# Gated recurrence of eight heads: output kept channel by token, its norm's sums made by products with ones, and a new table of deadline shifts

## The chip, the cores and the metric

The kernel runs on one core of one Trainium2 chip. The metric is the device time of one execution in microseconds, as the median of several runs. The kernel before took 1561.24 us (three runs, 1560.71 to 1561.47).

## The reference

One layer of a hybrid decoder on 1024 tokens of width 2048. `x` is normalised and multiplied with a combined weight `w_in`; its columns go to three groups: spatial gating in chunks of 128 tokens (gMLP), a gated delta rule with 8 heads of 128 channels, and attention into 256 memory tokens with 4 heads. Each group's output is multiplied with SiLU of its own gate columns, the three are joined, multiplied with `w_out`, added to `x`, and normalised again. The part that the change touches is the delta rule:

```python
q = l2norm(to_heads(q)) * DN_HEAD_DIM ** -0.5
k = l2norm(to_heads(k))
...
q_g = q * jnp.exp(g_cum)[..., None]
...
def step(state, inp):
    qg_c, kcd_c, val_c, ai_c, kd_c, gl_c = inp
    v_new = val_c - jnp.einsum('bhid,bhde->bhie', kcd_c, state)
    o_c = jnp.einsum('bhid,bhde->bhie', qg_c, state) + jnp.einsum('bhij,bhje->bhie', ai_c, v_new)
    state = state * jnp.exp(gl_c)[..., None, None] + jnp.einsum('bhid,bhie->bhde', kd_c, v_new)
    return state, o_c
...
o = rmsnorm(o, dn_norm_g[l]) * jax.nn.silu(d_z.reshape(B, S, DN_HEADS, DN_HEAD_DIM))
```

So each head's output `o` is normalised over its 128 channels, token by token, and each query is normalised to length one before it is used. The kernel runs the recurrence in chunks of 128 tokens.

## The kernel before

All tiles have 128 partitions. The 1024 tokens are worked on in two halves `hf` of 512 (`HT`), each of four chunks `tt` of 128.

**The big products.** The input projection, the memory's keys and values and the output projection are products of 128x128 by 128x512. Each factor is split into a high part (a cast to fp32r, on ScalarE, `S`) and a low part (a subtraction on VectorE, `V`), and three products stand for one (`triple`). `seven` arranges the blocks so that seven block products do the work of eight, which costs additions and subtractions of blocks on VectorE. Weights come in chunks into `raw`, and their parts stand in `rhi` and `rlo`, two of each; the left factors in `lh`, `ll`, `lm`.

**The order of work** is neither the order of the code nor found at run time. `Plan` records every operation with a cost that `price` gives it by engine and shape, builds the dependences from the tiles that are read and written, computes a due time for each operation from the end backwards (`late`), and lays the operations out in a simulated run (`lay`), each engine taking the ready operation with the earliest due time. `SHIFT` is a table by hand: it adds so many nanoseconds to the due times of single operations, which it names by their number. The result is a fixed sequence for each engine; at run time an engine only waits for semaphores. SyncE (`Q`, in the profile SP) issues nearly all DMAs, in its own fixed order. For ScalarE the plan knows that Exp, Silu and Gelu each need their own table (`FITS`), and books a load of it.

**The recurrence** is done in two parts for each pair of heads `p` and half `hf`, and both are worked in between the big products.

- `front` (line 1230): `conv` makes keys and queries, channel by token (128 channels on the partitions, 512 tokens). `qk` (line 1000) turns the keys to token by channel in PSUM (`to_tokens`: four TensorE transposes of 128x128) and sums their squares (`sumsq`: four ScalarE instructions that each square 128 columns and write the sum of a row). It then turns the queries in the same way for the sums of their squares, `hs[:, 0]`. It forms the products of keys with keys and queries with keys, and at last multiplies the queries by the row of decays that a DMA has put into a tile `vs` from `ring["tn"]`. Queries, keys, `kd` and `ai` go to HBM (`late_d`), the two norms that are still needed go to `late_hs`.
- `inverse` and `levels` invert the triangular matrices of four pairs at a time.
- `front_late` (line 1247) loads the tiles again, `values` makes the values, `back` runs four times `scan_step` (line 1170) and then `heads_out` (line 1211). `back_of` (line 1647) calls them. Pairs 0 and 1 (heads 0 to 3) are worked during the second projection stage, pairs 2 and 3 during the third.

In `scan_step` the output of a chunk is made token by channel, with the queries and then `ai` as the stationary operand:

```python
PE.matmul(d0, q, s, start=True, stop=False)
PE.matmul(d0, ai, w, start=first, stop=True)
```

and copied into `vs`. In `heads_out` the squares of a token stand in one row, so `sumsq` sums them in four instructions; one small VectorE operation adds the queries' term, `rsqrt_to` takes the power -1/2 on GpSimd, `by_token` scales the four chunks by it on ScalarE. Four transposes then turn the output to channel by token, in the bank that the scan used, and it is read from PSUM, multiplied by `dn_norm_g` and, for heads 4 to 7, by their gate (`g_d`), or stored to `o_d` until the gate of heads 0 to 3 is there.

Of the kernel before, what the change touches and what calls it, by code (L numbers as in the profile page):

```python
# [11 lines left out]
F32R = mybir.dt.float32r  # L12
AF = mybir.ActivationFunctionType
ALU = mybir.AluOpType
# [4 lines left out]
P = 128  # L19
# [18 lines left out]
KP = 4  # L38
ON_ACT = (3,)
NEG = -1.0e30  # L40
FITS = {AF.Exp: 1, AF.Silu: 2, AF.Gelu_apprx_tanh: 3}

# [21 lines left out]
class Plan:  # L64
# [8 lines left out]
    FETCH = 3500.0  # L73
    TABLE, HOLD = 1300.0, 6000.0
    SHIFT = {
# [5 lines left out]
    }  # L81

    def __init__(self, nc):
# [340 lines left out]
def kernel(  # L424
# [101 lines left out]
    ring["E"] = Ring("E", 2, [P, HT])  # L526
    ring["tn"] = Ring("tn", 4, [P, HT])
    ring["xr"] = Ring("xr", 3, [P, HT + 3])
    ring["hs"] = Ring("hs", 4, [P, 10, NT])
    jk = C([P, HT], "jk", mybir.dt.bfloat16)  # L530
    gr = C([NT * NH, P], "gr")
    small = Ring("small", 8, [P, 8])
# [8 lines left out]
    def tpb():  # L541
# [9 lines left out]
    G.affine_select(out=ident, in_=ident, compare_op=ALU.not_equal, fill=1.0, base=0,  # L551
                    pattern=[[-1, P]], channel_multiplier=1)
    G.memset(ones, 1.0)
    mhalf = C([P, 8], "mhalf")
    G.memset(mhalf, -0.5)
    with rank(0):
# [443 lines left out]
    def qk(h, hf, tiles, hs, gt, bank):  # L1000

        q, k = tiles[:2]
        kd, ai, vs = map(tok, (*tiles[2:4], ring["tn"]()))
        beta, edk = (scs[hf][:, i] for i in (0, 4))
        (kt,) = to_tokens((k, bank))
        sumsq(hs[:, 1], kt)
        V.tensor_scalar(hs[:, 1], hs[:, 1], EPS, None, op0=ALU.add)
        V.reciprocal(hs[:, 3], hs[:, 1])
        V.scalar_tensor_tensor(hs[:, 2], hs[:, 3], -1.0, beta[:, :, h], op0=ALU.mult, op1=ALU.mult)
        V.tensor_tensor(out=hs[:, 3], in0=hs[:, 2], in1=edk[:, :, h], op=ALU.mult)  # L1010
        by_token(kd, kt, hs[:, 3])
        e = tok(ring["E"]())
        Q.dma_start(e.rearrange("p t c -> p (t c)"), e_d[hf][h])
        Q.dma_start(vs.rearrange("p t c -> p (t c)"), row_of(ecs[hf], h))
        by_token(e, e, hs[:, 2])
        (qt,) = to_tokens((q, bank))
        sumsq(hs[:, 0], qt)
        V.tensor_scalar(hs[:, 0], hs[:, 0], P * EPS, P * EPS * EPS, op0=ALU.mult, op1=ALU.add)
        rsqrt_to(hs[:, 4], hs[:, 1])
        V.tensor_tensor(out=hs[:, 4], in0=hs[:, 4], in1=hs[:, 1], op=ALU.mult)  # L1020

        ch, cl = (ring["inv"](F32R).rearrange("p (t s c) -> p t s c", s=2, c=P) for _ in range(2))
        for i, src in enumerate((k, q)):
            split_to(ch[:, :, i], cl[:, :, i], tok(src), V)
        for t2 in range(NT // 2):
            d = bank
            for j in range(2):
                tt = 2 * t2 + j
                triple(d[:, j * 2 * P : (j + 1) * 2 * P], (ch[:, tt, 0], cl[:, tt, 0]), (ch[:, tt], cl[:, tt]),
                       True, True, R.cls)  # L1030
            dv = d.rearrange("p (t s c) -> p t s c", s=2, c=P)
            ts = slice(2 * t2, 2 * t2 + 2)
            V.tensor_tensor(out=gt[:, ts], in0=dv[:, :, 0], in1=e[:, ts], op=ALU.mult)
            V.tensor_tensor(out=ai[:, ts], in0=dv[:, :, 1], in1=e[:, ts], op=ALU.mult)
        V.tensor_tensor(out=q, in0=q, in1=vs.rearrange("p t c -> p (t c)"), op=ALU.mult)

    def blocks_out(gt, n):

# [131 lines left out]
    def scan_step(hf, hp, tt, qs, ks, rest, ut):  # L1170
# [12 lines left out]
        with rank(1):  # L1183
# [11 lines left out]
            with R.together():  # L1195
                if not last:
                    for s, q, k, kd, ai, vs, u, d0, d1, r, w, e, n in heads:
                        PE.matmul(d1, kd, w, start=True, stop=True)
                for s, q, k, kd, ai, vs, u, d0, d1, r, w, e, n in heads:
                    if not first:  # L1200
                        PE.matmul(d0, q, s, start=True, stop=False)
                    PE.matmul(d0, ai, w, start=first, stop=True)
            for s, q, k, kd, ai, vs, u, d0, d1, r, w, e, n in heads:
                if first:
                    V.tensor_copy(s, d1)
# [2 lines left out]
            for s, q, k, kd, ai, vs, u, d0, d1, r, w, e, n in heads:  # L1208
                S.copy(vs, d0)

    def heads_out(hf, hp, hss, rest):
        obs = [vs for kd, ai, vs in rest]

        for hs, ob in zip(hss, obs):
            sumsq(hs[:, 5], ob)
            V.scalar_tensor_tensor(hs[:, 6], hs[:, 5], 1.0 / P, hs[:, 0], op0=ALU.mult, op1=ALU.add)
            rsqrt_to(hs[:, 7], hs[:, 6])
            by_token(ob, ob, hs[:, 7])
        for h, ob, bank in zip(hp, obs, scan_banks):
            (tp,) = to_tokens((ob.rearrange("p t c -> p (t c)"), bank))  # L1220
            if h < NJ:
                S.activation(ob, tp, AF.Copy, scale=col2[:, 8:9])
                Q.dma_start(tok(o_d[hf][h]), ob)
            else:
                e, y = ring["E"](), ob.rearrange("p t c -> p (t c)")
                Q.dma_start(e, g_d[hf][h - NJ])
                V.scalar_tensor_tensor(ob, tp, col2[:, 8:9], tok(e), op0=ALU.mult, op1=ALU.mult)
                head_done(h, hf, y)

    def front(p, hf, banks):  # L1230

# [2 lines left out]
        for i, h in enumerate(hp):  # L1234
# [1 line left out]
            conv(1, h, hf, tiles[1])  # L1236
            conv(0, h, hf, tiles[0])
            qk(h, hf, tiles, hs, gt[:, i], banks[i])
            V.tensor_copy(late_hs[:, hf, h], hs[:, 0:5:4])
            for d, t in zip(late_d[hf][h], tiles[:4]):  # L1240
                Q.dma_start(d, t)
        gdr = blocks_out(gt, f"{hf}{p}")
# [4 lines left out]
    def front_late(p, hf):  # L1247

        hp = (2 * p, 2 * p + 1)
        qs, ks, hss, rest = [], [], [], []  # L1250
        for h, tiles in zip(hp, back_sets):
            hss.append(ring["hs"]())
            V.tensor_copy(hss[-1][:, 0:5:4], late_hs[:, hf, h])
            for d, t in zip(late_d[hf][h], tiles):
                Q.dma_start(t, d)
            qs.append(tiles[0])
            ks.append(tiles[1])
            rest.append([tok(t) for t in tiles[2:]])
        return hf, hp, qs, ks, hss, rest

    def values(hf, hp, qs, ks, hss, rest):
        for i, h in enumerate(hp):
            v = ring["tn"]()
            conv(2, h, hf, v)
            bank = scan_banks[i]
            by_token(rest[i][2], to_tokens((v, bank))[0], hss[i][:, 4])

    def back(hf, hp, qs, ks, hss, rest, ut):
        for tt in range(NT):
            scan_step(hf, hp, tt, qs, ks, rest, ut)  # L1270
        heads_out(hf, hp, hss, rest)


    late_hs = C([P, 2, NH, 2, NT], "lhs")

    def halves(t):
        n = t.shape[1] // 2
# [363 lines left out]
    project_stage(heads_of(NJ), to_heads(NJ), made=yu_d[0] if NA > 0 else None)  # L1641
    inv = inverse(gdrs, gg_d[0], "a", 1.9)
    front_sets = over([own_set])
    scan_banks = [dnr.bufs[0]] * 2
    gdrs = []

# [107 lines left out]
    scan_banks = dnr.bufs[0:2]  # L1754
    hand = dnr.bufs[3]
    wide = acc
    el = over([abh[:, 0:HT], ring["tn"].bufs.pop()])
    for hf in range(2):
        spatial(hf)
# [331 lines left out]
```

## Time and profile before

| what | value |
|---|---|
| runs | 1561.24 us median, 1560.71 to 1561.47 |
| profiled execution | 1558.44 us, its span 1556.70 us |
| granted TensorE clock | 0.998 |
| instructions | 25174 |
| HBM | 336.58 MB read, 100.40 MB written |

The span reaches from the first to the last instruction of the profiled execution; the execution's time has what lies around it as well. Nearly all instructions are recorded on line 420, the place where the plan issues them, so groups of instructions are told apart by their tiles: `dn<-ident,vs` is an operation that reads `ident` and `vs` and writes a PSUM bank `dn`; the names on the right are sorted by the alphabet and don't tell which operand is stationary. `acc` and `dn` are the two sets of four PSUM banks. A row of groups has count, busy time, mean length in ns, and the idle time of the engine ahead of it with what ended it. An fp32 product of 128x128 has two records, a transpose one. Lengths of TensorE instructions overlap; what one costs is read from the distance of starts.

### The profile page before, as it was taken

How to read it: one execution, taken by the hardware profiler on the slowest of the kernel's cores; microseconds unless marked ns; L12 is line 12 of the kernel's file. 1: busy time of each engine (PE TensorE's matmuls, PEld its weight loads, DVE VectorE, ACT ScalarE, POOL GpSimd, SP SyncE). 2: the span in 40 equal slices, each digit the busy share in tenths (PEclk: the TensorE clock that was granted, in tenths of full speed). 3: DMA queues.
4: the chain of work that ended last, by engine and by line, in shares of the span. 5: the costliest groups of instructions: out<-in, count | busy, mean ns of one | idle time of the engine just before them, and what ended most of it. 6: DMA issues, size and time to landing. Idle time of an engine off the chain costs nothing.

```text
span 1556.7 us, 25174 instructions
## 1 busy us (share of the span) xinstructions
PE 1546.4 (99%) x8725; PEld 1299.2 (83%) x8725; DVE 1250.4 (80%) x1843; ACT 947.8 (61%) x1942; POOL 102.0 (7%) x125
## 2 busy tenths in 40 slices
PE   9999999999999999999999999999999999999997
PEld 8988888888888888888888888888888888888886
DVE  6966974777898946788789975878758999998996
ACT  7833385565874335698885454776557874464554
POOL 0100000100021000010111010010000000000000
PEclk9999999999999999999999999999999999999999
DMA  9999976999879797786797987999958999775984
GB/s 326 308 303 332 310 258 220 308 329 311 297 248 296 239 276 223 265 281 198 260 327 270 326 242 230 310 328 333 346 208 271 314 333 328 268 254 198 342 276 174
DMA packets 348642, 438.68 MB, mean 282 GB/s; under 512 B 78553, under 2 KB 183394, under 8 KB 348514
## 3 DMA queue, kind: packets, MB, share of 16 engines
q1 hardware_dynamic: 346930, 434.37, 85.4%
q0 software_dynamic: 1088, 2.10, 0.5%
q8 instruction: 69, 1.13, 0.3%
q10 hardware_dynamic: 496, 0.61, 0.1%
q14 instruction: 59, 0.48, 0.1%
HBM read 336.58 MB, written 100.40 MB: 281 GB/s over the span
## 4 chain that ended last, share of the span: by engine, by line
PE 95%; DVE 3%; issue 1%; ACT 1%; DMA 0%; POOL 0%; POOLq 0%; SPq 0%; DVEq 0%; ACTq 0%
PE acc L420 60%; PE dn L420 35%; DVE rlo L420 1%; DVE ll L420 0%; DVE tn L420 0%; DVE obs L420 0%; DVE raw L420 0%; DVE inv L420 0%; DMA raw<-in_w_mem_kv_dram 0%; ACT E L420 0%; DVE rs L420 0%; DVE kept L420 0%; DVE xa L420 0%; ACT lh L420 0%; DVE small L420 0%
## 5 line engine op out<-in xcount | busy, mean ns | idle before, releaser
L420 PE MATMUL acc<-lh,rhi 128*128 128x512 f32 x1024 | 395.4, 395 | 0.0
L420 PE MATMUL acc<-lh,rlo 128*128 128x512 f32 x1024 | 384.8, 396 | 0.0
L420 ACT CAST rhi<-raw 128x1024 fp32r<-128x1024 f32 (+1 forms) x145 | 183.3, 1265 | 210.1 <-PE dn L420 106.6
L420 DVE TENSOR_TENSOR rlo<-raw,rhi 128x1024 fp32r<-128x1024 f32 (+1 forms) x145 | 215.5, 1486 | 95.8 <-ACT rhi L420 83.7
L420 PE MATMUL acc<-ll,rhi 128*128 128x512 f32 x688 | 267.1, 395 | 0.1
L420 PEld LDWEIGHTS acc<-lh,rhi 128*128 128x128 f32 x1024 | 192.3, 188 | 37.0 <-ACT qT L420 0.2
L420 PEld LDWEIGHTS acc<-lh,rlo 128*128 128x128 f32 x1024 | 191.6, 188 | 37.0
L420 PEld LDWEIGHTS acc<-ll,rhi 128*128 128x128 f32 x688 | 129.2, 188 | 25.1 <-DVE ll L420 0.6
L420 DVE TENSOR_TENSOR ll<-ll,lh 128x1024 fp32r<-128x1024 f32 x105 | 128.3, 1222 | 11.0 <-ACT lh L420 10.3
L420 PE MATMUL acc<-lm,rhi 128*128 128x512 f32 x336 | 131.6, 394 | 0.0
L420 ACT CAST lh<-ll 128x1024 fp32r<-128x1024 f32 (+1 forms) x107 | 111.5, 1043 | 23.8 <-PE dn L420 9.7
L420 PE MATMUL dn<-lh,rhi 128*128 128x512 f32 x288 | 112.6, 393 | 0.0
L420 PE MATMUL dn<-lh,rlo 128*128 128x512 f32 x288 | 110.8, 394 | 0.0
L420 PE MATMUL dn<-ll,rhi 128*128 128x512 f32 x192 | 75.1, 392 | 0.0
L420 DVE TENSOR_TENSOR rlo<-kept,rhi 128x1024 fp32r<-128x1024 f32 (+1 forms) x38 | 52.7, 1389 | 25.6 <-ACT rhi L420 25.5
L420 PEld LDWEIGHTS acc<-lm,rhi 128*128 128x128 f32 x336 | 63.2, 188 | 12.0
L420 ACT CAST rhi<-kept 128x1024 fp32r<-128x1024 f32 (+1 forms) x38 | 45.3, 1192 | 42.7 <-PE acc L420 25.4
L420 DVE TENSOR_TENSOR raw<-raw,kept 128x1536 f32<-128x1536 f32 (+1 forms) x42 | 64.3, 1532 | 3.2 <-DMA raw<-in_w_in_dram 2.3
L420 POOL TENSOR_TENSOR hs<-hs,mhalf 128x4 f32<-128x4 f32 x32 | 45.8, 1433 | 298.1 <-DVE hs L420 298.1
L420 PEld LDWEIGHTS dn<-lh,rhi 128*128 128x128 f32 x288 | 54.2, 188 | 10.2
L420 PEld LDWEIGHTS dn<-lh,rlo 128*128 128x128 f32 x288 | 54.1, 188 | 10.4
L420 POOL TENSOR_TENSOR small<-small,mhalf 128x1 f32<-128x1 f32 x26 | 19.7, 758 | 634.4 <-DVE small L420 634.4
(500 smaller groups left out, 3460.1 us busy)
## 6 DMA issues: line engine op xcount, KB each, us to landing
raw<-in_w_in_dram SPq DMA_DIRECT2D x168, 256.0 KB
raw<-in_w_in_dram SPq DMA_DIRECT2D x72, 512.0 KB
raw<-in_w_out_dram SPq DMA_DIRECT2D x64, 512.0 KB
ll<-hsd SPq DMA_DIRECT2D x54, 512.0 KB
lm<-hsd SPq DMA_DIRECT2D x26, 512.0 KB
pd<-obs SPq DMA_DIRECT2D x48, 256.0 KB
late<-os SPq DMA_DIRECT2D x44, 256.0 KB
ll<-h0d SPq DMA_DIRECT2D x18, 512.0 KB
```

Of the source, the lines that this page charges most:

```text
L420: o.fn(*o.args, **o.kw)
```

## The change

- `scan_step`: the operands of the two products for the output change places, so that it comes out channel by token.
- `heads_out`: the squares of queries and output (each with its scale, as 512 columns) are added on VectorE, split into a high and a low part, and summed over the channels by two TensorE products with a 128x128 tile of ones, `ones_r`, so that each of the 128 partitions holds the sum. A VectorE reciprocal of 128x512 out of PSUM and a ScalarE square root follow, and one VectorE product. There are no turns of the output and no GpSimd power. The tiles of queries, keys, `kd` and `ai` are used as working space.
- `qk`: the queries aren't turned, their squares not summed, and their product with the decay row is left out; `front_late` makes it, with the row loaded into a tile `faded` of its own, since `heads_out` needs the queries without decay.
- `front_late` takes its tiles from the rings anew each time, instead of from two fixed sets.
- `hs` and `late_hs` are half as large, `ones_r` is new, and `FITS` has the square root as a fourth table.
- `SHIFT` has 60 entries in place of 32, nearly all of them others.

```diff
--- before.py
+++ after.py
@@ -38,7 +38,7 @@
 KP = 4
 ON_ACT = (3,)
 NEG = -1.0e30
-FITS = {AF.Exp: 1, AF.Silu: 2, AF.Gelu_apprx_tanh: 3}
+FITS = {AF.Exp: 1, AF.Silu: 2, AF.Gelu_apprx_tanh: 3, AF.Sqrt: 4}

@@ -73,11 +73,14 @@
     FETCH = 3500.0
     TABLE, HOLD = 1300.0, 6000.0
     SHIFT = {
...
     }

     def __init__(self, nc):
@@ -526,7 +529,7 @@
     ring["E"] = Ring("E", 2, [P, HT])
     ring["tn"] = Ring("tn", 4, [P, HT])
     ring["xr"] = Ring("xr", 3, [P, HT + 3])
-    ring["hs"] = Ring("hs", 4, [P, 10, NT])
+    ring["hs"] = Ring("hs", 4, [P, 5, NT])
     jk = C([P, HT], "jk", mybir.dt.bfloat16)
     gr = C([NT * NH, P], "gr")
     small = Ring("small", 8, [P, 8])
@@ -551,6 +554,9 @@
     G.affine_select(out=ident, in_=ident, compare_op=ALU.not_equal, fill=1.0, base=0,
                     pattern=[[-1, P]], channel_multiplier=1)
     G.memset(ones, 1.0)
+    ones_r = C([P, P], "onesr", F32R)
+    with rank(0):
+        S.copy(ones_r, ones)
     mhalf = C([P, 8], "mhalf")
     G.memset(mhalf, -0.5)
     with rank(0):
@@ -1000,7 +1006,7 @@
     def qk(h, hf, tiles, hs, gt, bank):

         q, k = tiles[:2]
-        kd, ai, vs = map(tok, (*tiles[2:4], ring["tn"]()))
+        kd, ai = map(tok, tiles[2:4])
         beta, edk = (scs[hf][:, i] for i in (0, 4))
         (kt,) = to_tokens((k, bank))
         sumsq(hs[:, 1], kt)
@@ -1011,11 +1017,7 @@
         by_token(kd, kt, hs[:, 3])
         e = tok(ring["E"]())
         Q.dma_start(e.rearrange("p t c -> p (t c)"), e_d[hf][h])
-        Q.dma_start(vs.rearrange("p t c -> p (t c)"), row_of(ecs[hf], h))
         by_token(e, e, hs[:, 2])
-        (qt,) = to_tokens((q, bank))
-        sumsq(hs[:, 0], qt)
-        V.tensor_scalar(hs[:, 0], hs[:, 0], P * EPS, P * EPS * EPS, op0=ALU.mult, op1=ALU.add)
         rsqrt_to(hs[:, 4], hs[:, 1])
         V.tensor_tensor(out=hs[:, 4], in0=hs[:, 4], in1=hs[:, 1], op=ALU.mult)

@@ -1032,7 +1034,6 @@
             ts = slice(2 * t2, 2 * t2 + 2)
             V.tensor_tensor(out=gt[:, ts], in0=dv[:, :, 0], in1=e[:, ts], op=ALU.mult)
             V.tensor_tensor(out=ai[:, ts], in0=dv[:, :, 1], in1=e[:, ts], op=ALU.mult)
-        V.tensor_tensor(out=q, in0=q, in1=vs.rearrange("p t c -> p (t c)"), op=ALU.mult)

     def blocks_out(gt, n):

@@ -1198,8 +1199,8 @@
                         PE.matmul(d1, kd, w, start=True, stop=True)
                 for s, q, k, kd, ai, vs, u, d0, d1, r, w, e, n in heads:
                     if not first:
-                        PE.matmul(d0, q, s, start=True, stop=False)
-                    PE.matmul(d0, ai, w, start=first, stop=True)
+                        PE.matmul(d0, s, q, start=True, stop=False)
+                    PE.matmul(d0, w, ai, start=first, stop=True)
             for s, q, k, kd, ai, vs, u, d0, d1, r, w, e, n in heads:
                 if first:
                     V.tensor_copy(s, d1)
@@ -1208,24 +1209,29 @@
             for s, q, k, kd, ai, vs, u, d0, d1, r, w, e, n in heads:
                 S.copy(vs, d0)

-    def heads_out(hf, hp, hss, rest):
-        obs = [vs for kd, ai, vs in rest]
-
-        for hs, ob in zip(hss, obs):
-            sumsq(hs[:, 5], ob)
-            V.scalar_tensor_tensor(hs[:, 6], hs[:, 5], 1.0 / P, hs[:, 0], op0=ALU.mult, op1=ALU.add)
-            rsqrt_to(hs[:, 7], hs[:, 6])
-            by_token(ob, ob, hs[:, 7])
-        for h, ob, bank in zip(hp, obs, scan_banks):
-            (tp,) = to_tokens((ob.rearrange("p t c -> p (t c)"), bank))
+    def heads_out(hf, hp, raw_q, ks, rest):
+
+        for h, q, k, (kd, ai, vs), bank in zip(hp, raw_q, ks, rest, scan_banks):
+            o = vs.rearrange("p t c -> p (t c)")
+            S.activation(q, q, AF.Square, scale=math.sqrt(P * EPS))
+            S.activation(k, o, AF.Square, scale=1.0 / math.sqrt(P))
+            V.scalar_tensor_tensor(q, k, EPS * EPS, q, op0=ALU.add, op1=ALU.add)
+            hi, lo = ring["kd"](F32R), ring["ai"](F32R)
+            split_to(hi, lo, q, V)
+            with R.together():
+                PE.matmul(bank, ones_r, hi, start=True, stop=False)
+                PE.matmul(bank, ones_r, lo, start=False, stop=True)
+            V.reciprocal(k, bank)
+            S.activation(k, k, AF.Sqrt)
+            V.tensor_tensor(out=o, in0=o, in1=k, op=ALU.mult)
             if h < NJ:
-                S.activation(ob, tp, AF.Copy, scale=col2[:, 8:9])
-                Q.dma_start(tok(o_d[hf][h]), ob)
+                S.activation(o, o, AF.Copy, scale=col2[:, 8:9])
+                Q.dma_start(o_d[hf][h], o)
             else:
-                e, y = ring["E"](), ob.rearrange("p t c -> p (t c)")
+                e = ring["E"]()
                 Q.dma_start(e, g_d[hf][h - NJ])
-                V.scalar_tensor_tensor(ob, tp, col2[:, 8:9], tok(e), op0=ALU.mult, op1=ALU.mult)
-                head_done(h, hf, y)
+                V.scalar_tensor_tensor(o, o, col2[:, 8:9], e, op0=ALU.mult, op1=ALU.mult)
+                head_done(h, hf, o)

     def front(p, hf, banks):

@@ -1236,7 +1242,7 @@
             conv(1, h, hf, tiles[1])
             conv(0, h, hf, tiles[0])
             qk(h, hf, tiles, hs, gt[:, i], banks[i])
-            V.tensor_copy(late_hs[:, hf, h], hs[:, 0:5:4])
+            V.tensor_copy(late_hs[:, hf, h], hs[:, 4])
             for d, t in zip(late_d[hf][h], tiles[:4]):
                 Q.dma_start(d, t)
         gdr = blocks_out(gt, f"{hf}{p}")
@@ -1247,31 +1253,34 @@
     def front_late(p, hf):

         hp = (2 * p, 2 * p + 1)
-        qs, ks, hss, rest = [], [], [], []
-        for h, tiles in zip(hp, back_sets):
-            hss.append(ring["hs"]())
-            V.tensor_copy(hss[-1][:, 0:5:4], late_hs[:, hf, h])
+        qs, ks, vs, raw_q, rest = [], [], [], [], []
+        for i, h in enumerate(hp):
+            tiles = [ring[tag]() for tag in ("qT", "kT", "kd", "ai", "vs")]
             for d, t in zip(late_d[hf][h], tiles):
                 Q.dma_start(t, d)
-            qs.append(tiles[0])
+            q = faded()
+            Q.dma_start(q, row_of(ecs[hf], h))
+            V.tensor_tensor(out=q, in0=q, in1=tiles[0], op=ALU.mult)
+            raw_q.append(tiles[0])
+            qs.append(q)
             ks.append(tiles[1])
             rest.append([tok(t) for t in tiles[2:]])
-        return hf, hp, qs, ks, hss, rest
-
-    def values(hf, hp, qs, ks, hss, rest):
+        return hf, hp, qs, ks, raw_q, rest
+
+    def values(hf, hp, qs, ks, raw_q, rest):
         for i, h in enumerate(hp):
             v = ring["tn"]()
             conv(2, h, hf, v)
             bank = scan_banks[i]
-            by_token(rest[i][2], to_tokens((v, bank))[0], hss[i][:, 4])
-
-    def back(hf, hp, qs, ks, hss, rest, ut):
+            by_token(rest[i][2], to_tokens((v, bank))[0], late_hs[:, hf, h])
+
+    def back(hf, hp, qs, ks, raw_q, rest, ut):
         for tt in range(NT):
             scan_step(hf, hp, tt, qs, ks, rest, ut)
-        heads_out(hf, hp, hss, rest)
-
-
-    late_hs = C([P, 2, NH, 2, NT], "lhs")
+        heads_out(hf, hp, raw_q, ks, rest)
+
+
+    late_hs = C([P, 2, NH, NT], "lhs")

     def halves(t):
         n = t.shape[1] // 2
@@ -1641,6 +1650,7 @@
     project_stage(heads_of(NJ), to_heads(NJ), made=yu_d[0] if NA > 0 else None)
     inv = inverse(gdrs, gg_d[0], "a", 1.9)
     front_sets = over([own_set])
+    faded = ring["tn"]
     scan_banks = [dnr.bufs[0]] * 2
     gdrs = []

@@ -1754,6 +1764,7 @@
     scan_banks = dnr.bufs[0:2]
     hand = dnr.bufs[3]
     wide = acc
+    faded = over(own_set[0:2])
     el = over([abh[:, 0:HT], ring["tn"].bufs.pop()])
     for hf in range(2):
         spatial(hf)
```

13 rows, old and new, of the table SHIFT are left out of this document.

## The prediction

> **What bounds the kernel now.** I read the page first: busy shares, then the chain that ended last.
>
> ```profile
> PE 1546.4 (99%) x8725; PEld 1299.2 (83%) x8725; DVE 1250.4 (80%) x1843; ACT 947.8 (61%) x1942; POOL 102.0 (7%) x125
> PE 95%; DVE 3%; issue 1%; ACT 1%; DMA 0%; POOL 0%; POOLq 0%; SPq 0%; DVEq 0%; ACTq 0%
> ```
>
> TensorE is busy for all but 10.3 us of the span, and the chain is TensorE. But a busy PE need not be at its rate, so I went on to the windows, which also show who is next in line.
>
> ```profile
> core 0: us, PE busy (x) PEld busy (x) DVE busy (x) ACT busy (x) POOL busy (x), PEclk, DMA share, GB/s
> 624.00:897.00 273.00, 272.99 (x1443) 232.43 (x1442) 231.48 (x408) 197.41 (x527) 27.54 (x27) 1.00 0.84 276
> 897.00:975.00 78.00, 78.00 (x784) 64.12 (x783) 50.85 (x74) 38.22 (x59) 8.04 (x8) 1.00 0.81 237
> 975.00:1170.00 195.00, 195.00 (x1061) 167.34 (x1060) 146.59 (x217) 129.21 (x291) 15.04 (x13) 1.00 0.92 304
> 1170.00:1248.00 78.00, 77.93 (x405) 64.85 (x404) 68.45 (x111) 63.91 (x136) 0.00 (x0) 1.00 0.85 292
> 1248.00:1443.00 195.00, 194.81 (x869) 160.63 (x868) 184.90 (x219) 107.42 (x144) 0.00 (x0) 1.00 0.81 277
> ```
>
> The first two columns after the window are its length and PE's busy time. Heads 0 to 3 pass through the recurrence at 624:897 and heads 4 to 7 at 975:1170. PE waits there for nothing, at full granted clock. VectorE (DVE) stands at 85% and 75% of these stretches. In 1248:1443 DVE is filled to 95% and PE loses 0.19 us: a full DVE by itself doesn't starve PE.
>
> The rate comes from the chain and from a timeline of PE (start, length, group):
>
> ```profile
> 1313.38 21.76 PE acc L420 x96
> 664.97 0.40 PE L420 MATMUL acc<-lh,rlo 128*128 128x512 f32 x1
> 665.21 0.60 PE L420 MATMUL dn<-ident,os 128*128 128x128 f32 x4
> 665.57 0.48 PE L420 MATMUL acc<-lh,rhi 128*128 128x512 f32 x1
> 665.88 0.40 PE L420 MATMUL acc<-ll,rhi 128*128 128x512 f32 x1
> ```
>
> 96 products of 512 columns start every 21.76/96 = 0.227 us. From the start of the product ahead of a group of four transposes to the start of the second product behind it are 0.91 us; two products are 0.45, so the group costs PE 0.46 us, its switch to the next product (0.31 instead of 0.23) included. A transpose's length (0.27 us) is not its price, since four overlap.
>
> So PE issues without gaps, and what leaves its stream leaves the time, as long as the others keep up.
>
> The Trainium skill, "Perfetto Trace Analysis", section "Identifying the Most-Contended Engine", says to judge TensorE's headroom by the share of weight loading, not by matmul busy time. That is 83% here, which would leave a sixth of PE as slack. The trace speaks against it: a product starts every 0.227 us in the same stretch in which loading stands at 83%. Read that way the time wouldn't move; it is a rival below.
>
> **PE's part.** All counts are per head and half of the sequence, of which there are 16. Removed: the four transposes of the queries in `qk` and the four of the output in `heads_out`.
>
> ```profile
> L420 PE MATMUL dn<-ident,vs 128*128 128x128 f32 x64 | 9.4, 272 | 0.0
> L420 PE MATMUL dn<-states,qT 128*128 128x128 f32 x112 | 21.6, 275 | 0.0
> L420 PE MATMUL dn<-steps,ai 128*128 128x128 f32 x128 | 24.1, 275 | 0.0
> ```
>
> The first row is the output's turns: 64 = 16 x 4; the queries' are as many. 32 groups x 0.46 = 14.7 us removed; I take 0.45 for rounding, 14.4.
>
> Added: two products of `ones_r` with 512 columns, the shape of the row of 96: 32 x 0.227 = 7.3 us. They switch no shape. If each waited for ACT and for DVE at the price of the one switch above (0.08 us), that would be 32 x 0.08 = 2.6 more; a stream at 0.227 is the nearer row, so I take 0.5.
>
> In `scan_step` stationary and moving operand change places (second and third row), both 128x128, so the count and the shape stay. The newest operand, `w`, is already read by the product with `kd` ahead of it. Price: 0, at worst 0.08 us for each of 64 head-steps, 5 us; nothing in the rows suggests a gain.
>
> PE: -14.4 + 7.3 + 0.5 = **-6.6 us**.
>
> **ScalarE.**
>
> ```profile
> L420 ACT ACTIVATE jk<-dn 128x128 bf16<-128x128 f32 x128 | 36.9, 289 | 4.1 <-PE dn L420 2.1 <-DVE inv L420 0.8
> L420 ACT ACTIVATION_READ_ACCUMULATOR jk<-dn 128x1 f32 x128 | 27.5, 215 | 0.0
> L420 ACT ACTIVATE jk<-vs 128x128 bf16<-128x128 f32 x64 | 20.1, 314 | 0.8
> L420 ACT ACTIVATION_READ_ACCUMULATOR jk<-vs 128x1 f32 x66 | 12.8, 194 | 0.0
> L420 ACT ACTIVATE vs<-vs,hs 128x128 f32<-128x128 f32 x64 | 21.2, 400 | 2.2 <-POOL hs L420 2.2
> L420 ACT ACTIVATE obs<-obs 128x512 f32<-128x512 f32 x40 | 25.1, 635 | 13.6 <-DVE obs L420 13.5
> L420 ACT ACT_TABLE_LOAD x23 | 29.5, 1283 | 2.6 <-issue 2.2
> ```
>
> Removed: the queries' sums (half of the first two rows, 32.2 us), the output's (32.9) and its scaling by token (21.2): 86. Added: two squares, a cast and a root, each like the 635 ns row: 16 x 2.54 = 41 us. The root has its own table, and silu runs all through 624:897: up to two loads each time, one if the two heads share it, so 16 to 32 x 1.283 = 21 to 41 us. ACT comes out at -24 to -4 us, at 61% load: nothing.
>
> The Trainium skill, "ScalarE: Activation LUTs", section "Table sets: the hidden batching unit", speaks against this change: square roots sit in a set of their own, so calls should be batched by set. The trace has the load (1283 ns) but no root.
>
> **VectorE.**
>
> ```profile
> L420 DVE SCALAR_TENSOR_TENSOR os<-xr,cw,os 128x512 f32<-128x512 f32 x66 | 49.6, 754 | 1.5 <-ACT os L420 1.3
> L420 DVE TENSOR_TENSOR inv<-os,inv 128x512 fp32r<-128x512 f32 x22 | 14.8, 684 | 0.1
> L420 DVE TENSOR_TENSOR os<-os,tn 128x512 f32<-128x512 f32 x11 | 7.6, 688 | 6.8 <-PE dn L420 6.8
> L420 DVE TENSOR_SCALAR hs<-hs 128x4 f32<-128x4 f32 x32 | 5.0, 163 | 5.0 <-ACT jk L420 5.0
> L420 DVE RECIPROCAL hs<-hs 128x4 f32<-128x4 f32 x16 | 2.7, 170 | 0.0
> L420 DVE RECIPROCAL sc<-sc x2: 295/324/352, 160.8 to 161.1; 128x32 f32<-128x32 f32 x2
> ```
>
> Added: one sum (0.754), the low part of the split (0.684), a reciprocal of 128x512, and the product with it (0.688). No such reciprocal is in the trace. The last two rows have it at 4 elements (170 ns) and at 32 (295, 324, 352: shortest, median, longest): (324 - 170)/28 = 5.5 ns an element, and 0.17 + 508 x 0.0055 = 3.0 us. Bounds: 0.69 (as any operation of 512) and, by the longest, 0.17 + 508 x 0.0065 = 3.5; I take 3.0, since the slope is of the operation itself. The planner's `price` books (512 + 151)/0.96 = 691 ns, so its order runs ahead of DVE by some 2.3 us at each of the 16.
>
> The Trainium skill, "VectorE: DVE Perf Modes", section "First, the fixed hardware budget", has reciprocals divide with a repeat count of 8; as an estimate 512 x 8 / 0.96 GHz = 4.3 us.
>
> Removed: two operations on 128x4 (0.3). The product of q with its decay row (third row) stays but moves from `front` to `front_late`. Net 5.1 - 0.3 = 4.8 us x 16 = 77: DVE 1250 to about 1327, 85% of the span. By stretch: 624:897 holds 231.5 + 8 x 4.8 = 270 of 273; 975:1170 holds 146.6 + 8 x 4.8 + 8 x 0.69 (moved in) = 191 of 195. That is 99% and 98%: the place where the gain can be lost. Neighbours have room: 27 us in 897:975 and 10 in 1170:1248.
>
> **What else moves.**
>
> ```profile
> L420 POOL TENSOR_TENSOR hs<-hs,mhalf 128x4 f32<-128x4 f32 x32 | 45.8, 1433 | 298.1 <-DVE hs L420 298.1
> tn<-ecd SPq DMA_DIRECT2D x16, 256.0 KB
> L420 SPq DMA_DIRECT2D od<-vs x8: 319/329/820, 644.4 to 831.5; - x8
> L420 SPq DMA_DIRECT2D sm<-od x8: 385/424/1122, 652.5 to 842.3; - x8
> ```
>
> GpSimd loses half of the first row, 23 us, hidden anyway. The 16 decay rows are loaded in the late part; 8 come into 975:1170, 2.1 MB, 7 us at its 304 GB/s, its DMA share 0.92 to 0.96. SP issues in order, so such a load, waiting for its buffer, holds the weights queued behind it; they are loaded two chunks ahead, which hides a wait of a few us. The norm of one head is now a chain of 0.6 x 2 + 0.75 + 0.6 + 0.7 + 0.5 + 3.0 + 0.6 + 0.7 + 0.6, about 9 us, with tables 11, against about 6 (4 x 0.5 + 0.2 + 1.4 + 4 x 0.4 + 0.5 + 0.7). During it q, k, kd and ai now stay taken as well, so the next pair's loads start later. The last output stored (831.5) is read 10.8 us later (842.3), so 3 to 5 us are covered there; without that cover the gate's product would hold an accumulator and PE would wait those us.
>
> **The sum.** The profiled execution took 1558.44 us around its span of 1556.70: 1558.4 - 6.6 = 1551.8. The median of the runs is 2.8 above it (1561.24), so **1554.6 us**.
>
> **The rivals.**
>
> *VectorE becomes the bound (slower).* If DVE in 624:897 can't be filled beyond the 95% seen in 1248:1443, 270 us need 285: PE stands 12 us. Net +5, 1566 us; with the same in 975:1170 (191/0.95 = 201) it is +11, 1572. It decides where a reciprocal takes 3 us or more and nothing is shifted to the neighbours. For it: the planner's price. Against it: PE whole at 95%, and the room next door.
>
> *Half of it happens:* late weights cost PE 4 to 9 us, or the 5 us of the changed operand order come in: 1558 to 1564, no change that can be told.
>
> *PE isn't the bound* (weight loading 83%): 1561. Against it: the 0.227 us.
>
> **How the numbers follow.** Forecast 0.70; VectorE as bound 0.16; half 0.12; PE not the bound 0.02. About 0.2%, 3.1 us, is what a measurement of this kernel can tell from no change. So faster 0.70, same 0.14, slower 0.16. Range: below, the sum without the added waits is 1554.1, and if the new order takes some 50 more of the 0.08 us switches out of a stream of 8725, that is 4 us: 1550; above, it runs through the half case to 1563, leaving out the slower one.
>
> **What would show it.** PE: 128 records fewer and 32 more, 8629; busy about 1540, still 99%, idle some 10 us, no waits of PE for DVE above 1 us in 624:897. DVE about 1327 with 16 reciprocals near 3.0 us; 39 to 55 table loads; POOL half of the `hs` row. I am wrong if PE shows idle time or starts wider than 0.227 us in 624:897 or 975:1170 beside a DVE at 98% and more, or if head-steps cost PE more than before.

## The result, and the profile after

The changed kernel takes 1601.95 us (median of 5 runs, 1600.95 to 1603.73) against 1560.71 for the kernel before: a ratio of 1.0264, 95% interval 1.0249 to 1.0279. It is 41 us slower, where I forecast 6.6 us faster. Its profiled execution took 1601.17 us, with a span of 1599.4.

The page, after: busy time of each engine, and the shares of the chain that ended last:

```profile
PE 1554.9 (97%) x8629; PEld 1297.0 (81%) x8629; DVE 1323.4 (83%) x1859; ACT 949.3 (59%) x1706; POOL 81.3 (5%) x109
PE 80%; DVE 10%; issue 3%; ACT 2%; DMA 1%; POOLq 0%; POOL 0%; SPq 0%; ACTq 0%; DVEq 0%
```

The waits of TensorE, with who waits and on whom (sum in us, count, the longest):

```profile
PE dn L423 <- DVE kT L423: 13.2, 8, 2.6
PE dn L423 <- DVE hs L423: 5.2, 2, 2.6
PE acc L423 <- DVE lm L423: 3.1, 2, 1.9
PE dn L423 <- DVE lhs L423: 2.4, 1, 2.4
```

The count of 8629 TensorE records is the forecast one, and VectorE's busy time (1323 us, forecast 1327) and GpSimd's (21 us less, forecast 23) are near. But TensorE is idle for 44.5 us instead of 10.3, and VectorE has 10% of the chain, where it had 3% before. `kT` is the tile into which the reciprocal writes; `hs` and `lhs` are small operations that VectorE happens to do just behind one, so these lines name the same cause twice. The stretches, after, in the columns of before (the work comes later than before, by the waits ahead of it):

```profile
624.00:897.00 273.00, 255.20 (x1532) 211.68 (x1531) 249.68 (x400) 181.64 (x382) 16.27 (x17) 0.97 0.81 255
975.00:1170.00 195.00, 188.48 (x982) 159.38 (x982) 161.72 (x209) 116.49 (x196) 4.47 (x3) 1.00 0.84 279
1248.00:1443.00 195.00, 194.18 (x901) 160.83 (x900) 184.92 (x233) 123.59 (x197) 0.00 (x0) 1.00 0.87 297
```

TensorE waits 18 us in 624:897 with VectorE busy for 91% and 6.5 us in 975:1170 with VectorE at 83%, while 1248:1443, with VectorE at 95%, loses only 0.8 us (0.2 before). How full VectorE is doesn't say where TensorE waits. The new groups, after, do:

```profile
L423 DVE RECIPROCAL kT<-dn 128x512 f32<-128x512 f32 x16 | 53.5, 3347 | 0.2 <-PE dn L423 0.2
L423 PE MATMUL dn<-kd,onesr 128*128 128x512 f32 x16 | 6.7, 422 | 8.5 <-DVE hs L423 5.2 <-DVE kT L423 3.3
L423 PE MATMUL dn<-ai,onesr 128*128 128x512 f32 x16 | 6.4, 400 | 0.0
L423 ACT ACT_TABLE_LOAD x42 | 53.9, 1283 | 3.0 <-issue 2.2
```

A reciprocal takes 3.35 us, and the planner books 0.69. The timelines of TensorE and of VectorE show what stands behind it, at the first pair of heads:

```profile
649.58 0.40 PE L423 MATMUL acc<-lh,rhi 128*128 128x512 f32 x1
652.59 0.48 PE L423 MATMUL dn<-kd,onesr 128*128 128x512 f32 x1 [2.61 <-DVE hs L423]
653.60 1.51 PE L423 MATMUL acc<-lh,rhi 128*128 128x512 f32 x4
657.52 1.11 PE L423 MATMUL dn<-ident,tn 128*128 128x128 f32 x4 [2.42 <-DVE lhs L423]
658.81 0.79 PE L423 MATMUL dn<-lh,rhi 128*128 128x512 f32 x1 [0.17 <-DVE obs L423]
659.40 0.63 PE L423 MATMUL dn<-ll,rhi 128*128 128x512 f32 x1
659.83 0.63 PE L423 MATMUL dn<-lh,rlo 128*128 128x512 f32 x1
```

```profile
647.22 1.29 DVE L423 TENSOR_TENSOR ai<-qT,kd 128x512 fp32r<-128x512 f32 x2
649.09 3.36 DVE L423 RECIPROCAL kT<-dn 128x512 f32<-128x512 f32 x1
652.44 1.75 DVE L423 TENSOR_TENSOR rlo<-raw,rhi 128x1536 fp32r<-128x1536 f32 x1
654.11 3.35 DVE L423 RECIPROCAL kT<-dn 128x512 f32<-128x512 f32 x1
658.07 0.68 DVE L423 TENSOR_TENSOR obs<-dn,ym 128x512 f32<-128x512 f32 x1
```

The reciprocal reads the sums out of a PSUM bank. At this stage both heads of a pair share one bank (`scan_banks` names the same buffer twice), so the second head's product with ones (652.59) has to wait until the first head's reciprocal has ended (652.45), though the low parts of both heads, its last operands, are done at 648.51. The next pair's turns of the values (657.52) wait until the second's has ended (657.46). TensorE works in order, so the products behind them wait too. In the whole trace ten waits of TensorE, 20.6 us together, end within 0.2 us behind the end of a reciprocal. The others are for operands from a late VectorE, such as `lm` at 1209 us, just behind a reciprocal, and `lm` at 843 and `ll` at 1027, some 5 to 8 us behind one, or they occur with a short instruction as well (next section), such as the 1.3 us for `steps`.

These waits bring something else: from 659.40 on, products start 0.43 us apart instead of 0.23. The windows show the granted clock (the column ahead of the DMA share):

```profile
640.00:654.00 14.00, 11.39 (x59) 9.34 (x58) 13.67 (x20) 12.12 (x26) 1.38 (x1) 1.00 0.84 271
654.20:660.80 6.60, 4.01 (x12) 2.50 (x11) 6.60 (x8) 3.43 (x6) 0.00 (x0) 0.50 0.57 187
661.00:675.00 14.00, 14.00 (x74) 11.86 (x73) 13.30 (x20) 12.52 (x32) 0.00 (x0) 1.00 0.89 282
708.70:712.10 3.40, 3.40 (x10) 2.63 (x9) 3.40 (x2) 0.83 (x3) 0.00 (x0) 0.50 0.77 269
```

In this profile the clock is halved at 654.1 (for 6.83 us) and at 708.7, 845.2, 971.5 and 1210.4 (for 3.41 us each), 20 us in all ahead of the kernel's end, and each time TensorE had idled for 1.6 to 2.6 us of the 3.41 us just ahead. Eight products start in 3.4 us at 0.43 us, where 0.23 would give fifteen.

### The profile page after: what moved, and what is told of

It reads as the page before. It is cut to its first block, busy times and chain, and to the rows that moved or that the text cites. A ratio compares the mean times of both kernels' runs of the same rounds, so it can differ in the third digit from the quotient of the medians.

```text
span 1599.4 us, 24825 instructions
## 1 busy us (share of the span) xinstructions
PE 1554.9 (97%) x8629; PEld 1297.0 (81%) x8629; DVE 1323.4 (83%) x1859; ACT 949.3 (59%) x1706; POOL 81.3 (5%) x109
## 4 chain that ended last, share of the span: by engine, by line
PE 80%; DVE 10%; issue 3%; ACT 2%; DMA 1%; POOLq 0%; POOL 0%; SPq 0%; ACTq 0%; DVEq 0%
PE acc L423 51%; PE dn L423 29%; DVE kT L423 3%; DVE rlo L423 1%; DVE ll L423 1%; DVE raw L423 1%; DVE tn L423 1%; ACT vs L423 0%; ACT rhi L423 0%; ACT E L423 0%; DVE os L423 0%; DVE ai L423 0%; DVE obs L423 0%; DVE lm L423 0%; DVE inv L423 0%
## 5 line engine op out<-in xcount | busy, mean ns | idle before, releaser
L423 PE MATMUL acc<-lh,rlo 128*128 128x512 f32 x1024 | 390.1, 397 | 0.8 <-DVE rlo L423 0.8
L423 PE MATMUL acc<-rhi,lh 128*128 128x512 f32 x144 | 56.0, 392 | 0.3 <-ACT lh L423 0.3
```

What stands on the lines that cost most here:

```text
L423: o.fn(*o.args, **o.kw)
```

## Experiments

All times are medians; a ratio is to the kernel before, measured beside it (1559 to 1560 us). Theory A: the order was made for a reciprocal of 0.69 us, and TensorE waits for banks and operands that come 2.66 us late, sixteen times. The rivals: B, VectorE has too much to do there in any order; C, the tables of the square root; D, the table of shifts or the exchanged operands.

**The reciprocal made short, in the same order.** A copy of the same shape is booked like the reciprocal, so all five engines keep the order of the changed kernel, instruction for instruction. It leaves the inversion out.

```diff
-            V.reciprocal(k, bank)
+            V.tensor_copy(k, bank)
```

> The changed kernel with the reciprocal of 128x512 (3.35 us in its profile) replaced by a copy of the same shape, which the planner books at the same 691 ns: the order of every engine is the same, only the 16 long instructions are short. It leaves the inversion out. Theory A (the static order was made for 0.69 us and TensorE waits at the banks and low parts that stand behind the 3.35 us): nearly all of the loss goes, 1554 us as predicted, within 1552 to 1558. Theory B (VectorE has too much work in these stretches, whatever the order): it goes as well, 1554 to 1560, so this run alone doesn't part A from B. Theory C (square root tables and ScalarE): 1585 to 1602. Theory D (the table of shifts or the exchanged operands make a bad order): 1585 to 1602.

Measured: 1560.9 us, ratio 1.0011 (1.0002 to 1.0020). The loss is gone, to 1.7 us, and the time lies just above the ranges that A (1552 to 1558) and B (1554 to 1560) gave. The same place of the two timelines, with the copy:

```profile
649.55 0.40 PE L423 MATMUL acc<-lh,rhi 128*128 128x512 f32 x1
649.87 0.47 PE L423 MATMUL dn<-kd,onesr 128*128 128x512 f32 x1
652.20 0.65 PE L423 MATMUL dn<-ident,tn 128*128 128x128 f32 x4 [0.24 <-DVE kT L423]
653.73 0.50 PE L423 MATMUL dn<-lh,rhi 128*128 128x512 f32 x1 [0.88 <-DVE obs L423]
```

The product with ones starts 2.72 us earlier in its place, and the turns have 0.24 us of wait instead of 2.42. So in this order the 41 us hang on the length of these 16 instructions. But the 6.6 us that I forecast don't appear either; that is taken up below.

**The square root's tables.** The root is replaced by ScalarE's identity, which the planner books like the root; this leaves the root out.

```diff
-FITS = {AF.Exp: 1, AF.Silu: 2, AF.Gelu_apprx_tanh: 3, AF.Sqrt: 4}
+FITS = {AF.Exp: 1, AF.Silu: 2, AF.Gelu_apprx_tanh: 3, AF.Identity: 4}
-            S.activation(k, k, AF.Sqrt)
+            S.activation(k, k, AF.Identity)
```

> The changed kernel with the square root replaced by ScalarE's identity, which the planner books like the root (its own table and 6 us of hold), so the order is the same, but no table for the root is loaded. It leaves the root out. Theories A and B: table loads fall from 42 to about 25 and the time moves by less than 6 us, 1596 to 1602. Theory C: 1560 to 1585.

Measured: 1601.16 us, ratio 1.0267 (1.0247 to 1.0288), with 27 table loads instead of 42. Fifteen loads of 1.28 us fewer make no difference that can be told; C falls. (TensorE idles 42.5 us instead of 44.5, but its clock is halved for 27 us instead of 20.)

**How the wait grows with the length.** Half of the columns, still booked at 0.69 us (`R.pin`), in the same order; half of the inversion is left out:

```diff
-            V.reciprocal(k, bank)
+            R.pin = True; V.reciprocal(k[:, 0:256], bank[:, 0:256]); R.pin = False
```

> The changed kernel, its order kept instruction for instruction, with the reciprocal over 256 of the 512 columns (1.75 us instead of 3.35, still booked at 0.69). It leaves half of the inversion out. The copy (0.68) gave 1561, the whole reciprocal 1602. If each reciprocal's excess goes to TensorE as a whole: 1561 + 16 x 1.07 = 1578. If TensorE has a lead of about a microsecond, and the half-rate clock after waits of 2 to 3 us is part of the loss: 1563 to 1570.

Measured: 1572.22 us, ratio 1.0080 (1.0063 to 1.0097). The group of the reciprocal in this run:

```profile
L425 DVE RECIPROCAL kT<-dn 128x256 f32<-128x256 f32 x16 | 27.9, 1748 | 0.2 <-PE dn L425 0.2
```

And the window that ran at half clock in the changed kernel:

```profile
654.20:660.80 6.60, 4.83 (x22) 3.89 (x23) 6.60 (x12) 5.43 (x10) 0.00 (x0) 1.00 0.92 295
```

Three points of one order: 0.68, 1.75 and 3.35 us a reciprocal give ratios of 1.0011, 1.0080 and 1.0264. The first 16 x 1.07 = 17 us cost 11 us (two thirds: TensorE has some lead), the next 16 x 1.6 = 26 us cost 29, more than the whole. The surplus goes with the halved clock: with waits of half the length it doesn't occur before the kernel's end. The pages of the copy, the half and the whole begin:

```profile
PE 1542.6 (99%) x8629; PEld 1291.9 (83%) x8629; DVE 1282.5 (82%) x1859; ACT 949.1 (61%) x1706; POOL 83.8 (5%) x109
PE 1546.1 (98%) x8629; PEld 1292.1 (82%) x8629; DVE 1297.2 (83%) x1859; ACT 949.0 (60%) x1706; POOL 86.0 (5%) x109
PE 1554.9 (97%) x8629; PEld 1297.0 (81%) x8629; DVE 1323.4 (83%) x1859; ACT 949.3 (59%) x1706; POOL 81.3 (5%) x109
```

Taken from the spans (1558.7, 1570.7, 1599.4), TensorE idles 16.1, 24.6 and 44.5 us. So of the 41 us between the first and the last, 28 are idle time; TensorE is busy for 17.6 us at half clock, which is some 9 us more than at full clock, by my estimate. The time lay between my two expectations, 1578 and 1563 to 1570.

**The true price.** One more line in `price`, the change else untouched; then also without the table of shifts.

```diff
+            if name == "reciprocal":
+                o.cost = 150.0 + 6.25 * n
```

> The changed kernel with one more line in the planner's price: a reciprocal is booked at 150 + 6.25 ns an element (3350 ns for 512), the table of shifts kept. VectorE has the same work as in the changed kernel. Theory A: the order now leaves room, most of the loss returns, 1555 to 1568. Theory B: the work is unchanged, so 1585 to 1602. The shifts were set for another order, so some 10 us above the best are possible under A.

> As the run with the true price, with the table of shifts empty. Theory A: 1558 to 1575, the difference to the run with the table is what the table is worth here, either sign. Theory B: 1585 and more.

Measured: 1592.12 us with the table, ratio 1.0212 (1.0195 to 1.0229), and 1585.24 without, 1.0167 (1.0152 to 1.0182). Both lie in the ranges of B (1585 to 1602; 1585 and more), the second at its edge, and above those of A. But a booking alone, with the same work, recovers 10 or 17 of the 41 us, for which B has no reason. To see what an order loses without its table, three more runs had the table emptied: the kernel before, the changed kernel, and the run with the copy.

```diff
-    SHIFT = {...}
+    SHIFT = {}
```

> The kernel before with its table of shifts empty. Theory A2 (the static order only runs without waits once its due times have been adjusted; what the truly priced reciprocal still loses is mostly that): 1572 to 1585, so that the run with the true price and no table (1585, 26 us above the kernel before) is no worse than this. Theory B2 (the long reciprocals cost even in an order that knows them, since VectorE works in order and everything behind one waits 3.35 us): 1559 to 1566, with the run at the true price some 20 us above it.

> The changed kernel with its table of shifts empty and the reciprocal still booked at 0.69 us. If the table is the cause of the loss (theory D) this is well below the changed kernel's 1602; if the table was only worth something for short reciprocals it is 1590 to 1602; if it helped in spite of them, 1602 to 1620. Against the run with the true price and no table (1585) it gives what the booking alone costs: 10 to 25 us by theory A, under 5 by B2.

> The changed kernel with a copy in place of the reciprocal (booked 0.69 us, runs 0.68) and the table of shifts empty; it leaves the inversion out. Against the run with the true price and no table (1585) it has the same instructions but for 16 x 2.66 us on VectorE. Theory A2: within 8 us of it, 1577 to 1585. Theory B2: 1558 to 1570.

Measured, as ratios (us):

| | with its table | no table |
|---|---|---|
| kernel before | 1 (1559 to 1561) | 1.0022, 1.0012 to 1.0031 (1563.22) |
| changed kernel | 1.0264 (1601.95) | 1.0341, 1.0326 to 1.0357 (1612.42) |
| with the copy | 1.0011 (1560.90) | 1.0076, 1.0061 to 1.0091 (1571.40) |
| reciprocal at its true price | 1.0212 (1592.12) | 1.0167 (1585.24) |

The table helps the changed kernel and the copy by 10 us each, and it harms the order with the true price: it fits the order made for 0.69 us. D falls as far as the table goes. Without tables, the long reciprocal costs 41 us when it is booked short (1612 against 1571) and 14 when it is booked truly (1585 against 1571). Theory A has 27 us of the 41. The other 14 are what B2 expected: the kernel before hardly needs its table, and the copy's 1571 is 1 us above B2's range. Whether they are VectorE's time is asked next.

**What the other 14 are.** First the bank: ScalarE takes the root out of PSUM, VectorE inverts it in SBUF, so the bank is free after one ScalarE operation. Then the length: four pieces, between which the planner may put other work. Both have the true price and no table.

```diff
-            V.reciprocal(k, bank)
-            S.activation(k, k, AF.Sqrt)
+            S.activation(k, bank, AF.Sqrt)
+            V.reciprocal(k, k)
```

> The run with the true price and no table (1585), with root and reciprocal exchanged: ScalarE takes the square root out of the PSUM bank, VectorE inverts it in SBUF. The bank is free after some 0.6 us instead of 3.35, VectorE's work is the same. If what is left with the true price is TensorE waiting for the bank that the reciprocal holds: 1570 to 1577 (the 1571 of the copy without table, and a little). If it is the other VectorE work queued behind the 3.35 us: 1581 to 1588.

```diff
-            V.reciprocal(k, bank)
+            for tt in range(NT):
+                V.reciprocal(k[:, tt * P : (tt + 1) * P], bank[:, tt * P : (tt + 1) * P])
```

> The run with the true price and no table (1585), with the reciprocal in four pieces of 128 columns, each booked at 950 ns. VectorE has slightly more work (16 x 0.4 us), but nothing has to wait more than 1 us behind a piece, as the planner may put other work between them; the bank is held at least as long. If the long instruction in an in-order queue is what is left: 1570 to 1578. If it is the bank, or the sum of VectorE's work: 1582 to 1590.

Measured: 1590.92, ratio 1.0203 (1.0188 to 1.0218), and 1581.70, 1.0148 (1.0133 to 1.0163). With the bank freed sooner the kernel is 6 us slower, and with pieces 3 us faster. The first is outside both of its ranges; the second falls 0.3 us short of the 1582 to 1590 for the bank or the sum of VectorE's work. But each of these runs has an order of its own, so neither decides, and the next one kept the order of the true price, instruction for instruction, and put the copy in place of the reciprocal (`R.pin` has it booked at the reciprocal's 150 + 6.25 n ns); it leaves the inversion out.

```diff
-            V.reciprocal(k, bank)
+            R.pin = True; V.tensor_copy(k, bank); R.pin = False
```

> The run with the true price and no table (1585), its order kept instruction for instruction, with the copy in place of the reciprocal (the planner books the copy at 3350 ns as well). It leaves the inversion out. If the 14 us that the true price leaves against the copy without table (1571) are VectorE's real time, in an order that knows it: 1566 to 1574. If they are the order that the planner makes around a long instruction: 1581 to 1586.

Measured: 1581.41, ratio 1.0143 (1.0128 to 1.0158), as expected if the order is the cause (1581 to 1586). In an order that knows about it, the 43 us of VectorE time that were taken away are worth 4 us. What is left is the order itself. Its stretch 975:1170:

```profile
975.00:1170.00 195.00, 187.57 (x993) 158.96 (x993) 153.98 (x226) 124.16 (x218) 3.92 (x4) 0.97 0.90 291
```

TensorE stands 7 us here with VectorE at 79%, and the clock falls again. So B, too much work for VectorE, falls as the main cause: with the same copy in both, the order that the planner lays around a long instruction is 10 us slower than the one around a short (1581 against 1571, both without table). Why it is slower I haven't tested.

**The exchanged operands**, on top of the run with the copy:

```diff
-                        PE.matmul(d0, s, q, start=True, stop=False)
-                    PE.matmul(d0, w, ai, start=first, stop=True)
+                        PE.matmul(d0, q, s, start=True, stop=False)
+                    PE.matmul(d0, ai, w, start=first, stop=True)
```

> The run with the copy in place of the reciprocal (1560.9), with the two products of the recurrence's output in the operand order of the kernel before; planner and order are the same. It leaves the inversion out and makes the output of a chunk turned. My prediction's price of the exchange was 0: 1560.9 within 1.5 us. If the exchange cost its upper bound of 5 us, 1556.

Measured: 1560.91 us, ratio 1.0006 (0.9996 to 1.0015). The exchange is free, and with that the rest of D falls.

**The norm without VectorE's reciprocal.** ScalarE has a reciprocal square root. In the run with the copy it replaces the root, so the whole norm is computed again; then it reads the bank itself, with the table of shifts (each entry kept on its operation) and without. In all three the function takes the root's place in `FITS`.

```diff
-            V.reciprocal(k, bank)
-            S.activation(k, k, AF.Sqrt)
+            V.tensor_copy(k, bank)
+            S.activation(k, k, AF.Abs_reciprocal_sqrt)
```

> The changed kernel with the copy in place of the reciprocal, and ScalarE's reciprocal square root in place of the square root: planner, order and table of shifts are those of the run with the copy (1560.9), but the norm is computed in full again. Theory A: 1560.9 within 1.5 us. If ScalarE takes longer for this function, 1562 to 1570.

```diff
-            V.reciprocal(k, bank)
-            S.activation(k, k, AF.Sqrt)
+            S.activation(k, bank, AF.Abs_reciprocal_sqrt)
```

> As the run before, without the copy: ScalarE's reciprocal square root reads the PSUM bank, and VectorE has no part in it. The table of shifts is kept, each entry on the operation that it was made for; the order changes a little, since VectorE loses 16 operations of 0.69 us. The predicted saving on TensorE is 6.6 us, and the run with the copy gave 7 us of it back in nine waits: 1554 to 1563.

> The run in which ScalarE's reciprocal square root reads the bank (1577.5), with the table of shifts empty. If that run was slow because the table's entries belong to another order: 1562 to 1572. If VectorE's missing copies make the order itself worse: 1577 and more.

Measured: 1560.82, ratio 1.0008 (0.9999 to 1.0018); 1577.51, 1.0119 (1.0104 to 1.0134); 1570.55, 1.0075 (1.0060 to 1.0090). The first repairs the change: it computes the same as the changed kernel, 41 us faster. It doesn't beat the kernel before. The second has sixteen operations fewer on VectorE (1274 us busy instead of 1282) and is 17 us slower than the first, where I expected 1554 to 1563: the planner lays another order, to which the table's entries do harm (7 us) and which has waits of its own. That ScalarE, with its table loads, now holds the bank may have a part in them; no run parts the two. With the same copy, two orders differed by 10 us above, which is more than the change could have gained.

## Why the prediction was wrong, point by point

**PE's part: right as a term.** I had -6.6 us. The distances between starts, summed over the whole trace without the waits in them, fall by some 5.4 us from the kernel before to the run with the copy. The 128 transposes fewer and 32 products more are there as counted, and the operand exchange costs nothing, as measured.

**"What leaves its stream leaves the time, as long as the others keep up": the gain was lost there even with the short reciprocal.** By the pages, TensorE is busy for 3.8 us less in that run than before (1542.6 against 1546.4) and idles 5.8 us more (16.1 against 10.3), which gives the 2.0 us by which its span (1558.7) is longer. The new waits lie at 68, 450, 652, 714 and 1290 us, so a part of them far from the norm. Without tables TensorE idles 13.1 us in the kernel before and 23.3 with the copy.

**VectorE: the price was nearly right, its consequence wrong. This is the step that failed.** I took 3.0 us, bounds 0.69 to 3.5; measured 3.35. I even wrote that the planner's order runs ahead of VectorE by some 2.3 us at each of the 16. Sixteen times 2.66 us is 42.6 us, and the kernel lost 41. I didn't carry that line into the sum. I took the share of time that VectorE is busy as what decides, priced the slower rival from it ("It decides where a reciprocal takes 3 us or more and nothing is shifted to the neighbours", 1566 to 1572), and counted on 95% full stretches that lose nothing. But a stretch in which VectorE is full by plan and TensorE waits for nothing says nothing of an operation that is long against the plan. I granted the reciprocal a lead without asking what stands directly behind it on TensorE. That was to be read from the code: the products with ones write the bank that it reads, and `scan_banks` gives both heads one bank.

**The rivals.** VectorE as the bound had the right engine and instruction and the wrong mechanism: not its share (91% and 83%), but the lateness of single instructions in a static order. Its price, 5 to 11 us, was at most a quarter of the measured. The times of "half of it happens" (1558 to 1564) and "PE isn't the bound" (1561) didn't come. The run with the copy has such a time, but by the waits of a new order, which neither of them named, and no run shows a slack of TensorE behind its 83% of weight loading. I left out the clock: no stretch that I showed has it below 1.00, since TensorE hardly idled between its first product and its last.

**ScalarE, GpSimd, the DMAs: off in part, without weight.** ACT is busy for 949 us (forecast 924 to 944, before 948): the lengths of its instructions fell by 24 us in sum, as forecast, but the short ones that went had overlapped. It has 42 loads (39 to 55), worth nothing in time. GpSimd's `hs` row is halved (45.8 to 24.1 us). The DMA share of 975:1170 fell from 0.92 to 0.84 where I forecast 0.96, and TensorE waited for a DMA only once, 0.2 us. VectorE's total is near by two errors: the reciprocals took 5.5 us more than forecast (53.5 against 48), the rest 9 us less.

**What stays open.** Why the planner's orders with the true price, and the one without VectorE's part, have 10 to 20 us of scattered waits. For the true price the runs show that it is the order and not VectorE's work; which of the planner's decisions, they don't. For the kernel without VectorE's part the order isn't parted from ScalarE's hold on the bank.

## What to carry to other kernels

In a kernel whose order is fixed by a cost model, price every new instruction against the model's own formula first: where it is longer than booked, the excess times the count is a first forecast (43 us here, for 41), and a lead at that place makes it less (17 us for 11). Ask of each new PSUM reader what TensorE does next with that bank. And where one engine is busy for 99%, a small saving on it can be worth less than what a newly laid order loses, as here 3.8 us less busy time against 5.8 us more idle time; whether a change of 0.4% gains is known only when the new order has run.

## What the runs showed of the hardware

VectorE's reciprocal costs 6.25 to 6.5 ns an element: 0.91 us at 128 columns, 1.75 at 256, 3.35 at 512, where a copy of 512 takes 0.68. ScalarE's reciprocal square root takes no longer than its square root:

```profile
L423 ACT ACTIVATE kT<-kT 128x512 f32<-128x512 f32 x21 | 13.1, 635 | 5.1 <-DVE kT L423 4.7
```

(16 of the 21 are the reciprocal square roots, in the run with the copy; the other five are silu. With the copy and the square root the row also has 635.)

TensorE's clock is halved for 3.4 us or a multiple after waits that are shorter than that: at 709 it followed 2.6 us of idling, at 845 1.2 us in one wait and 1.6 us within the 3.4 us ahead. Other waits, of 2.22 us (776) and 2.55 us (1076), had no such effect. The five times in the changed kernel lie 16, 40, 37 and 70 times 3.413 us apart. Cut into windows of that length from there, its trace has five windows with 1.9 us or more of idling, all followed by half clock, four with about 1.6 us, of which one is, and none with less that is. The Trainium skill, "TensorE: Matmul & The Clock Gate", section "What's actually happening", describes windows of about 3.4 us that run freely, in which the activity decides on half or full clock; that fits the lengths seen here and that the same wait sometimes counts and sometimes doesn't. The Trainium skill has in the same page, section "HAM oscillation — how this bites in real kernels", the rule that idle gaps above some 3.4 us are to be avoided; here 1.6 us were enough.
